# Streaming the high and low activation parts as one 512-column matmul in a two-part float32r trunk

## The chip, the cores and the metric

The kernel runs on one core of one Trainium2 chip, as one launch. The metric is the device time of that launch in microseconds (us); lower is better. Engines are named as in the profile: PE is TensorE's matmuls, PEld its weight loads, DVE is VectorE, ACT is ScalarE, POOL is GpSimd, SP issues most DMAs.

## The reference

Two layers of a decoder trunk over 256 tokens with 1024 features, in float32. Each layer is a half-step SwiGLU feed-forward, a mixer (dilated attention beside a gated linear recurrence), a cross-attention into 256 memory tokens, and a second half-step feed-forward; an RMS norm stands ahead of each and at the end.

```python
def swiglu(h, w_gu, w_down):
    gate, up = jnp.split(h @ w_gu, 2, axis=-1)
    return (jax.nn.silu(gate) * up) @ w_down
...
    for l in range(DEPTH):
        x = x + 0.5 * swiglu(rms_norm(x, ffn1_norm[l]), ffn1_w_gu[l], ffn1_w_down[l])
        h = rms_norm(x, mix_norm[l])
        z = h @ w_in[l]
        ...
        merged = jax.nn.sigmoid(gate_a) * y_a + jax.nn.sigmoid(gate_b) * y_b
        x = x + merged @ w_mix_out[l]
        x = x + cross_attention(rms_norm(x, xattn_norm[l]), rms_norm(mem, mem_norm[l]),
                                xattn_wq[l], xattn_wkv[l], xattn_wo[l])
        x = x + 0.5 * swiglu(rms_norm(x, ffn2_norm[l]), ffn2_w_gu[l], ffn2_w_down[l])
    return rms_norm(x, final_norm)
```

Nearly all arithmetic is in the products of 256 tokens with weight matrices: 67 million weights in all, each used once.

## The kernel before, in words

**Two-part arithmetic.** Every weight and every activation operand is held as a high part (the value rounded to float32r) and a low part (the rest). A product is three matmuls that add into the same place of PSUM: high by high, high by low, low by high (`mm3`).

**Weights.** All weights lie in DRAM as blocks of 128 x 128 in the order of their use. `Stream` loads them in chunks of 16 blocks (1 MB), and splits them in halves of 8 blocks: ACT casts a half to `whi` (L104), DVE subtracts to get `wlo` (L110). Each time that a half is begun, `take` prepares later halves and then calls `tick`.

**Two kinds of products.** A feature-major product (`fm`) keeps a 128 x 128 weight block standing in the array and streams a tile of activations, 128 features by 256 tokens; its output tile has 128 output features by 256 tokens. L259 is high weight by high activation, L260 the same high weight by the low activation, L261 low weight by high activation. There are 3840 weight blocks in such products. A token-major product (`tm`, L263 to L265) keeps activations standing and streams four weight blocks at once, 512 columns; there are 224 matmuls of each of its three lines.

**Order of the work around them.** The order is written by hand. `defer(n, f)` puts a function off by n ticks, that is by n halves; `sides` holds side work (the recurrence `hgrn`, the attention heads, cross-attention scores, memory norms), of which a tick runs one step; `urgent` holds the norms, and evictions queue behind it. So the stream of matmuls on PE is a row of `fm` and `tm` blocks with small groups of side matmuls between halves. `Act` keeps high and low parts of an operand in separate tiles. Most `fm` calls compute two output tiles of 16 blocks in all; the down projections one tile of 22 blocks.

**PSUM.** There are eight banks of 128 x 512, taken one at a time by `bank()`. An `fm` output tile uses the first 256 columns of a bank. The eviction reads it straight: in the feed-forward, DVE multiplies by the norm (L423, L425), ACT applies SiLU (L424), DVE multiplies (L428), ACT rounds (L243) and DVE subtracts (L246). L353 adds a product to the residual.

Of the kernel before, what the change touches and what calls it, by code (L numbers as in the profile page):

```python
# [46 lines left out]
class Stream:  # L47
    """Weight blocks of 128 x 128 in the order of their use: loaded in chunks, split in high and low parts."""
# [16 lines left out]
    def pieces(self, i, before=None):  # L65
        """Both parts of half i, by pairs of blocks."""
# [46 lines left out]
    def take(self, descs):  # L113
        """The parts of the next blocks, which lie side by side."""
# [13 lines left out]
def build(tc, a, nchunks):  # L128
# [11 lines left out]
    psum = ent(tc.tile_pool(name="psum", bufs=8, space=bass.MemoryType.PSUM))  # L140
# [7 lines left out]

    def bank():
        return psum.tile([P, 512], F32, name="bank")  # L150
# [68 lines left out]
    class Row:  # L219
        """Tiles of [128, 256], four to a slot; a slot is taken when it is first asked for."""  # L220
# [8 lines left out]

    class Act:  # L230
        """A feature-major operand in two parts; tile k holds features 128 k .. 128 k + 127 of all tokens."""

        def __init__(self):
            self.h, self.l = Row(F32R), Row(F32R)

        def hi(self, k):
            return self.h(k)

        def lo(self, k):
            return self.l(k)  # L240

        def put(self, k, src, later=0):
            nc.scalar.copy(self.hi(k), src)  # L243

            def low():
                nc.vector.tensor_tensor(self.lo(k), src, self.hi(k).bitcast(F32), op=OP.subtract)  # L246
# [29 lines left out]
    def fm(name, l, cols, act, K, evac):  # L276
        """Feature-major products: one output tile of 128 columns of the weight for each of cols."""
        banks = [bank() for _ in cols]
        for k in range(K):
            for c, b in zip(cols, banks):  # L280
                wh, wl = W.take([(name, l, k * P, c)])
                mm3(b[:, :T], wh, wl, act.hi(k), act.lo(k), k == 0, k == K - 1, True)
        after(lambda: evac(*[b[:, :T] for b in banks]))

    def tm(name, l, c, act, evac):
        """Token-major products: 512 columns of the weight, both tiles of tokens."""
        banks = [bank(), bank()]
# [54 lines left out]
    class Resid:  # L342
        """Takes the products that are added to the residual, and makes the next operand of them."""
# [6 lines left out]
        def take(self, j, *ps):  # L350
            js = range(j, j + len(ps))
            for j, p in zip(js, ps):
                nc.vector.scalar_tensor_tensor(xt[j], p, self.scale, xt[j], op0=OP.mult, op1=OP.add)  # L353
            for j in js:
                self.act.put_gain(j, xt[j], self.gain(j))
            for j in js:
                self.norm.add(xt[j])

    class Last:
        """Takes the last products, and returns the normed residual, token-major."""  # L360
# [5 lines left out]
        def take(self, j, p):  # L366
            nc.vector.scalar_tensor_tensor(xt[j], p, 0.5, xt[j], op0=OP.mult, op1=OP.add)
# [14 lines left out]
        def turn(self, j, g):  # L382
            for i in range(2):
                if (i, j // 4) not in self.b:
                    self.b[i, j // 4] = bank()
                nc.tensor.transpose(self.b[i, j // 4][:, (j % 4) * P:(j % 4 + 1) * P], g[:, i * P:(i + 1) * P], ident)

        def finish(self, g):
# [10 lines left out]
            for i in range(2):  # L399
                o = slot()  # L400
                nc.scalar.activation(o[:, :512], self.b[i, 0], AF.Copy, scale=r[:, i:i + 1])
                nc.vector.tensor_scalar(o[:, 512:], self.b[i, 1], r[:, i:i + 1], None, op0=OP.mult)
# [3 lines left out]
    def mm_resid(name, l, act, K, res):  # L406
        if K == KD:
            for j in range(0, KD, 2):
                fm(name, l, [j * P, (j + 1) * P], act, K,
                   lambda p, q, j=j: res.take(j, p, q))  # L410
        else:
            for j in range(KD):
                fm(name, l, [j * P], act, K, lambda p, j=j: res.take(j, p))

# [1 line left out]
    def ffn(pre, l, res, nxt):  # L416
# [3 lines left out]
        for j in range(KF):  # L420
            def evac(pg, pu, j=j):
                g, s, u = tmp(), tmp(), tmp()
                nc.vector.tensor_tensor(g, pg, n.bc, op=OP.mult)  # L423
                nc.scalar.activation(s, g, AF.Silu)  # L424
                nc.vector.tensor_tensor(u, pu, n.bc, op=OP.mult)  # L425

                def stage2():
                    nc.vector.tensor_tensor(u, s, u, op=OP.mult)  # L428
                    act.put(j, u, later=0 if j == KF - 1 else 1)
                if j == KF - 1:  # L430
                    stage2()
                else:
                    defer(1, stage2)
            fm(pre + "_w_gu", l, [j * P, FF + j * P], h, KD, evac)
# [86 lines left out]
    def hgrn(l, hh, Q, K, F, ib, sog, out):  # L521
# [63 lines left out]
        bs = []  # L585
        for i in range(2):
            b = bank()
            bs.append(b)
# [35 lines left out]
    def attention(l, h, qk, v, out):  # L624
        b0, b1, b2 = bank(), bank(), bank()
# [359 lines left out]
```

## Time and profile before

| | |
|---|---|
| time, median of 3 runs | 1681.54 us (1681.42 to 1681.98) |
| span of the profiled execution, first to last instruction | 1679.6 us |
| median less that span | 1.9 us |
| PE busy | 1666.9 us (99%) |
| DVE busy | 1120.2 us (67%) |
| ACT busy | 836.9 us (50%) |
| POOL busy | 63.8 us (4%) |

The table's own time for the profiled execution is its span; the time of a run is a little longer than the span. "Busy" of PE counts overlapping records of a pipeline (a matmul's record starts before the one ahead of it has ended), so the distance between starts, not the record's length, says how fast matmuls follow each other.

### The profile page before, as it was taken

How to read it: one execution, taken by the hardware profiler on the slowest of the kernel's cores; microseconds unless marked ns; L12 is line 12 of the kernel's file. 1: busy time of each engine (PE TensorE's matmuls, PEld its weight loads, DVE VectorE, ACT ScalarE, POOL GpSimd, SP SyncE). 2: the span in 40 equal slices, each digit the busy share in tenths (PEclk: the TensorE clock that was granted, in tenths of full speed). 3: DMA queues.
4: the chain of work that ended last, by engine and by line, in shares of the span. 5: the costliest groups of instructions: out<-in, count | busy, mean ns of one | idle time of the engine just before them, and what ended most of it. 6: DMA issues, size and time to landing. Idle time of an engine off the chain costs nothing.

```text
span 1679.6 us, 34164 instructions
## 1 busy us (share of the span) xinstructions
PE 1666.9 (99%) x14658; PEld 1625.1 (97%) x14658; DVE 1120.2 (67%) x1821; ACT 836.9 (50%) x1285; POOL 63.8 (4%) x85
## 2 busy tenths in 40 slices
PE   8999999999999999999999999999999999999998
PEld 8999998899999999999999999988999999999998
DVE  7766586667768667666566656867586777676654
ACT  5554435555555555444444444445565555554442
POOL 2000000111100000000000000010110000000000
PEclk9999999999999999999999999999999999999999
DMA  7544444444455445554545544444344554445551
GB/s 282 191 177 176 178 175 153 150 176 151 151 177 180 175 147 176 181 192 180 183 174 193 179 178 174 162 148 174 146 157 154 192 197 155 149 178 180 192 180 76
DMA packets 41767, 289.42 MB, mean 172 GB/s; under 512 B 4880, under 2 KB 5008, under 8 KB 7440
## 3 DMA queue, kind: packets, MB, share of 16 engines
q1 hardware_dynamic: 41328, 286.73, 47.6%
q8 instruction: 114, 1.87, 0.4%
q10 hardware_dynamic: 288, 0.52, 0.1%
q14 instruction: 37, 0.30, 0.0%
HBM read 286.18 MB, written 1.05 MB: 171 GB/s over the span
## 4 chain that ended last, share of the span: by engine, by line
PE 98%; DVE 1%; DMA 0%; SPq 0%; ACT 0%; issue 0%; POOLq 0%; POOL 0%; ACTq 0%; DVEq 0%
PE bank L259 28%; PE bank L261 28%; PE bank L260 28%; PE bank L263 3%; PE bank L265 3%; PE bank L264 3%; PE bank L547 1%; PE bank L669 1%; PE bank L632 1%; PE bank L592 0%; DMA raw<-w 0%; PE bank L628 0%; PE bank L671 0%; PE bank L329 0%; DVE wlo L77 0%; PE bank L836 0%
## 5 line engine op out<-in xcount | busy, mean ns | idle before, releaser
L259 PE MATMUL bank<-slot,whi 128*128 128x256 f32 x3840 | 1095.0, 285 | 0.0
L261 PE MATMUL bank<-slot,wlo 128*128 128x256 f32 x3840 | 1087.0, 283 | 2.9 <-DVE wlo L77 2.9
L260 PE MATMUL bank<-slot,whi 128*128 128x256 f32 x3840 | 1086.8, 283 | 0.0
L261 PEld LDWEIGHTS bank<-slot,wlo 128*128 128x128 f32 x3840 | 736.4, 192 | 4.1 <-DVE wlo L77 4.1
L260 PEld LDWEIGHTS bank<-slot,whi 128*128 128x128 f32 x3840 | 736.6, 192 | 1.3
L259 PEld LDWEIGHTS bank<-slot,whi 128*128 128x128 f32 x3840 | 736.5, 192 | 1.5
L110 DVE TENSOR_TENSOR wlo<-raw,whi 128x1024 fp32r<-128x1024 f32 x532 | 648.7, 1233 | 39.1 <-ACT whi L104 35.0
L104 ACT CAST whi<-raw 128x1024 fp32r<-128x1024 f32 x532 | 540.9, 1043 | 58.0 <-PE bank L260 23.9
L423 DVE TENSOR_TENSOR tmp<-bank,bc 128x256 f32<-128x256 f32 x88 | 37.4, 425 | 157.0 <-PE bank L261 153.0
L424 ACT ACTIVATE tmp<-tmp 128x256 f32<-128x256 f32 x88 | 36.8, 420 | 201.8 <-DVE tmp L423 201.8
L243 ACT CAST slot<-tmp 128x256 fp32r<-128x256 f32 x152 | 60.4, 407 | 109.2 <-DVE tmp L428 38.5
L253 ACT ACTIVATE slot<-x,vecs 128x256 fp32r<-128x256 f32 x64 | 30.8, 505 | 138.5 <-DVE x L353 136.3
L263 PE MATMUL bank<-whi,slot 128*128 128x512 f32 x224 | 90.0, 402 | 0.0
L265 PE MATMUL bank<-whi,slot 128*128 128x512 f32 x224 | 87.5, 390 | 0.0
L264 PE MATMUL bank<-wlo,slot 128*128 128x512 f32 x224 | 87.4, 390 | 0.0
L353 DVE SCALAR_TENSOR_TENSOR x<-bank,x 128x256 f32<-128x256 f32 x56 | 22.7, 425 | 85.6 <-PE bank L261 85.6
L760 DVE TENSOR_TENSOR slot<-bank,cosb 128x256 f32<-128x256 f32 x48 | 20.4, 425 | 64.4 <-ACT tmp L759 62.9
L246 DVE TENSOR_TENSOR slot<-tmp,slot 128x256 fp32r<-128x256 f32 x152 | 60.9, 419 | 2.8 <-ACT slot L243 2.8
L265 PEld LDWEIGHTS bank<-whi,slot 128*128 128x128 f32 x224 | 42.0, 188 | 9.2
L761 POOL TENSOR_TENSOR tmp<-tmp,sinb 128x256 f32<-128x256 f32 x48 | 35.4, 740 | 391.7 <-ACT tmp L759 390.7
L263 PEld LDWEIGHTS bank<-whi,slot 128*128 128x128 f32 x224 | 42.1, 188 | 8.3
L264 PEld LDWEIGHTS bank<-wlo,slot 128*128 128x128 f32 x224 | 42.2, 188 | 7.7
(178 smaller groups left out, 973.9 us busy)
## 6 DMA issues: line engine op xcount, KB each, us to landing
raw<-w SPq DMA_DIRECT2D x267, 1024.0 KB, 4.8
slot<-mem SPq DMA_DIRECT2D x6, 512.0 KB, 7.1
x<-x SPq DMA_DIRECT2D x4, 256.0 KB, 4.8
raw<-w SPq DMA_DIRECT2D x4, 256.0 KB, 5.2
cst<-cst SPq DMA_DIRECT2D x1, 721.0 KB, 11.6
y<-slot ACTq DMA_DIRECT2D x2, 256.0 KB, 2.8
y<-slot SPq DMA_DIRECT2D x2, 256.0 KB, 2.8
posi<-positions SPq DMA_DIRECT2D x1, 128.0 KB, 10.5
```

Source lines behind the costliest of these rows:

```text
L104: nc.scalar.copy(self.hi[i], r)
L110: nc.vector.tensor_tensor(self.lo[i], r, self.hi[i].bitcast(F32), op=OP.subtract)
L243: nc.scalar.copy(self.hi(k), src)
L246: nc.vector.tensor_tensor(self.lo(k), src, self.hi(k).bitcast(F32), op=OP.subtract)
L259: nc.tensor.matmul(out, wh, ah, start=first, stop=False)
L260: nc.tensor.matmul(out, wh, al, start=False, stop=False)
L261: nc.tensor.matmul(out, wl, ah, start=False, stop=last)
L263: nc.tensor.matmul(out, ah, wh, start=first, stop=False)
L264: nc.tensor.matmul(out, ah, wl, start=False, stop=False)
L265: nc.tensor.matmul(out, al, wh, start=False, stop=last)
L423: nc.vector.tensor_tensor(g, pg, n.bc, op=OP.mult)
L424: nc.scalar.activation(s, g, AF.Silu)
```

## The change

The two activation parts of a tile now lie side by side in a slot (`Act.parts`, 512 columns), and `fm` streams both past the standing high weight in one matmul of 512 columns (L320 of the new kernel). Its output fills a whole bank: the left half takes high by high, the right half high by low. The low weight then adds its product with the high activations to the left half (L321, 256 columns). The eviction has to add the two halves: `add_halves` copies the right half to SBUF on ACT (L327) at once, and one tick later DVE adds the left half to it (L330); what followed before (norm, SiLU and so on) now follows that sum, in joint operations of two tiles. For products that go to the residual, two scalar_tensor_tensor operations take the place of one. PSUM is handed out in four pairs of banks, and a `bank()` for side work takes a pair as well.

```diff
+    joins = ent(tc.tile_pool(name="joins", bufs=4))
-    psum = ent(tc.tile_pool(name="psum", bufs=8, space=bass.MemoryType.PSUM))
+    psum = ent(tc.tile_pool(name="psum", bufs=4, space=bass.MemoryType.PSUM))
...
+    def pair():
+        return psum.tile([P, 1024], F32, name="pair")
+
     def bank():
-        return psum.tile([P, 512], F32, name="bank")
+        return pair()[:, :512]
...
-    def fm(name, l, cols, act, K, evac):
-        banks = [bank() for _ in cols]
-        for k in range(K):
-            for c, b in zip(cols, banks):
-                wh, wl = W.take([(name, l, k * P, c)])
-                mm3(b[:, :T], wh, wl, act.hi(k), act.lo(k), k == 0, k == K - 1, True)
-        after(lambda: evac(*[b[:, :T] for b in banks]))
+    def fm(items, evac):
+        b = pair().rearrange("p (i h t) -> p i h t", i=2, h=2)
...
+        for k, i in order:
+            name, l, c, act, K = items[i]
+            wh, wl = W.take([(name, l, k * P, c)])
+            nc.tensor.matmul(b[:, i], wh, two(act.parts(k)), start=k == 0, stop=False)
+            nc.tensor.matmul(b[:, i, 0], wl, act.hi(k), start=False, stop=k == K - 1)
+        n = len(items)
+        after(lambda: evac(b[:, :n, 0], b[:, :n, 1]))
+
+    def add_halves(d, left, right, then, now=False):
+        nc.scalar.copy(d, right)
+        def add():
+            nc.vector.tensor_tensor(d, left, d, op=OP.add)
+            then()
+        if now:
+            add()
+        else:
+            defer(1, add)
...
-                nc.vector.scalar_tensor_tensor(xt[j], p, self.scale, xt[j], op0=OP.mult, op1=OP.add)
+            for half in (left, right):
+                nc.vector.scalar_tensor_tensor(x, half, self.scale, x, op0=OP.mult, op1=OP.add)
...
-                nc.vector.tensor_tensor(g, pg, n.bc, op=OP.mult)
-                nc.scalar.activation(s, g, AF.Silu)
-                nc.vector.tensor_tensor(u, pu, n.bc, op=OP.mult)
+                t, s = join(), tmp()
+                u = t[:, T:]
+                def stage1():
+                    nc.vector.tensor_tensor(two(t), two(t), both(n.bc), op=OP.mult)
+                    nc.scalar.activation(s, t[:, :T], AF.Silu)
...
+                add_halves(two(t), left, right, stage1, last)
```

On PE, inside any feed-forward product, two weight blocks stood like this before (`slot` is the activation operand, `whi` and `wlo` the weight parts):

```order
100 L259 MATMUL bank<-slot,whi 128x256
101 L260 MATMUL bank<-slot,whi 128x256
102 L261 MATMUL bank<-slot,wlo 128x256
103 L259 MATMUL bank<-slot,whi 128x256
104 L260 MATMUL bank<-slot,whi 128x256
105 L261 MATMUL bank<-slot,wlo 128x256
```

and the same two blocks stand like this in the changed kernel:

```order
78 L320 MATMUL pair<-slot,whi 128x512
79 L321 MATMUL pair<-slot,wlo 128x256
80 L320 MATMUL pair<-slot,whi 128x512
81 L321 MATMUL pair<-slot,wlo 128x256
```

Six matmuls with six weight loads have become four with four; the streamed columns, 768 a block, are the same.

On DVE, while the recurrence's first pass (`hgrn`, whose steps update Q and K in L553 and L554) runs between the products of the forget gate and the query (`recur`: L708, L710, L713, L714), one pair of output tiles came with these rows before:

```order
267 L708 TENSOR_TENSOR tmp<-bank,bc 128x256
268 L710 SCALAR_TENSOR_TENSOR slot<-bank,bc 128x256
269 L110 TENSOR_TENSOR wlo<-raw,whi 128x1024
270 L713 TENSOR_SCALAR slot<-tmp,oml,lb 128x256
271 L714 TENSOR_SCALAR slot<-slot 128x256
272 L553 TENSOR_TENSOR slot<-slot,tt 128x32x16
273 L554 TENSOR_TENSOR slot<-slot,tt 128x32x16
274 L557 TENSOR_TENSOR tt<-tt 128x32
275 L563 COPY_PREDICATED tmp<-cpm,bank 128x8x16
276 L110 TENSOR_TENSOR wlo<-raw,whi 128x1024
```

In the changed kernel the same pair's rows, here with the next step of the recurrence behind them, are these (L764, L766, L770, L771, L609, L610 and L613 are the old L708, L710, L713, L714, L553, L554 and L557):

```order
285 L330 TENSOR_TENSOR join<-pair,join 128x512
286 L764 TENSOR_TENSOR join<-join,bc 128x256
287 L766 SCALAR_TENSOR_TENSOR slot<-join,bc 128x256
288 L110 TENSOR_TENSOR wlo<-raw,whi 128x1024
289 L770 TENSOR_SCALAR slot<-join,oml,lb 128x256
290 L771 TENSOR_SCALAR slot<-slot 128x256
291 L609 TENSOR_TENSOR slot<-slot,tt 128x16x32
292 L610 TENSOR_TENSOR slot<-slot,tt 128x16x32
293 L613 TENSOR_TENSOR tt<-tt 128x16
```

The pair has one more DVE row, the addition of 512 columns out of PSUM, and the four others have moved back by one half of weights.

On ACT, a feed-forward pair stood like this before (L104 casts weights, L307 squares for the memory norm):

```order
58 L307 ACTIVATE tmp<-slot 128x256
59 L424 ACTIVATE tmp<-tmp 128x256
60 L104 CAST whi<-raw 128x1024
61 L243 CAST slot<-tmp 128x256
62 L104 CAST whi<-raw 128x1024
```

and stands like this now (L360, L480 and L275 are the old L307, L424 and L243):

```order
66 L360 ACTIVATE tmp<-slot 128x256
67 L327 COPY join<-pair 128x512
68 L104 CAST whi<-raw 128x1024
69 L480 ACTIVATE tmp<-join 128x256
70 L104 CAST whi<-raw 128x1024
71 L275 CAST slot<-join 128x256
```

The copy of the right halves is new and stands ahead of the weight cast; SiLU has moved behind that cast.

## Rows read from the trace of the kernel before

**Rows 1.** The page: span, busy engines, and the chain's shares by engine.

```profile
span 1679.6 us, 34164 instructions
...
PE 1666.9 (99%) x14658; PEld 1625.1 (97%) x14658; DVE 1120.2 (67%) x1821; ACT 836.9 (50%) x1285; POOL 63.8 (4%) x85
...
PE 98%; DVE 1%; DMA 0%; SPq 0%; ACT 0%; issue 0%; POOLq 0%; POOL 0%; ACTq 0%; DVEq 0%
```

**Rows 2.** All waits of PE: who waited for whom, us in total, times, longest.

```profile
PE bank L261 <- DVE wlo L77: 2.9, 6, 0.5
PE bank L209 <- ACT warm L206: 2.3, 1, 2.3
PE bank L393 <- ACT tmp L372: 0.8, 1, 0.8
```

**Rows 3.** Timeline of PE in the feed-forward: start, duration in us, line, shape.

```profile
799.74 0.28 PE L260 MATMUL bank<-slot,whi 128*128 128x256 f32 x1
...
805.98 0.28 PE L261 MATMUL bank<-slot,wlo 128*128 128x256 f32 x1
```

**Rows 4.** Timeline of PE in a token-major product, and where it ends.

```profile
262.12 0.40 PE L264 MATMUL bank<-wlo,slot 128*128 128x512 f32 x1
...
265.98 0.39 PE L263 MATMUL bank<-whi,slot 128*128 128x512 f32 x1
...
270.09 0.39 PE L265 MATMUL bank<-whi,slot 128*128 128x512 f32 x1
270.31 0.28 PE L259 MATMUL bank<-slot,whi 128*128 128x256 f32 x1
270.43 0.28 PE L260 MATMUL bank<-slot,whi 128*128 128x256 f32 x1
```

**Rows 5.** Timeline of PE: attention scores in plain float32, six records merged.

```profile
326.28 1.46 PE L632 MATMUL bank<-slot 128*128 128x256 f32 x6
```

**Rows 6.** Groups by line and shape: busy us, mean ns of one, idle before.

```profile
L259 PE MATMUL bank<-slot,whi 128*128 128x256 f32 x3840 | 1095.0, 285 | 0.0
...
L110 DVE TENSOR_TENSOR wlo<-raw,whi 128x1024 fp32r<-128x1024 f32 x532 | 648.7, 1233 | 39.1 <-ACT whi L104 35.0 <-PE bank L261 2.0 <-issue 1.4
...
L423 DVE TENSOR_TENSOR tmp<-bank,bc 128x256 f32<-128x256 f32 x88 | 37.4, 425 | 157.0 <-PE bank L261 153.0 <-ACT bc L331 4.0
...
L605 DVE TENSOR_TENSOR slot<-bank,rs 128x512 f32<-128x512 f32 x8 | 5.1, 681 | 0.0
...
L660 ACT COPY slot<-bank 128x512 f32<-128x512 f32 x8 | 4.7, 584 | 9.8 <-PE bank L657 9.6
```

**Rows 7.** Busy us of PE, PEld, DVE, ACT, POOL in stretches; clock, DMA share, GB/s.

```profile
37.00:47.00 10.00, 10.00 (x85) 10.00 (x84) 7.85 (x15) 4.88 (x7) 0.00 (x0) 1.00 0.48 170
...
212.00:482.00 270.00, 269.99 (x2750) 254.96 (x2749) 188.71 (x305) 137.44 (x213) 21.95 (x28) 1.00 0.44 158
...
235.00:239.00 4.00, 4.00 (x136) 3.84 (x133) 3.97 (x9) 2.31 (x3) 0.00 (x0) 1.00 0.21 88
239.00:243.00 4.00, 4.00 (x126) 3.80 (x114) 4.00 (x9) 0.44 (x2) 0.00 (x0) 1.00 0.43 111
```

**Rows 8.** Timeline of DVE through one pair of the recurrence's products.

```profile
234.61 0.42 DVE L708 TENSOR_TENSOR tmp<-bank,bc 128x256 f32<-128x256 f32 x1 [1.15 <-PE bank L261]
...
237.70 0.69 DVE L554 TENSOR_TENSOR slot<-slot 128x512 f32<-128x512 f32 x1
238.30 0.68 DVE L557 TENSOR_TENSOR tt<-slot 128x512 f32<-128x512 f32 x1
...
242.07 0.45 DVE L708 TENSOR_TENSOR tmp<-bank,bc 128x256 f32<-128x256 f32 x1
```

**Rows 9.** The chain of work that ended last, at a step of the recurrence.

```profile
238.66 0.67 PE bank L547 x52
```

**Rows 10.** Timelines: PE's last paced matmul at the start; the last residual update.

```profile
16.64 0.38 PE L261 MATMUL bank<-slot,wlo 128*128 128x256 f32 x1 [0.49 <-DVE wlo L77]
...
1671.00 0.42 DVE L367 SCALAR_TENSOR_TENSOR x<-bank,x 128x256 f32<-128x256 f32 x1 [6.53 <-PE bank L261]
```

More of the change, by code (lines that the diff above doesn't have):

```diff
@@ L147, in tmp, with join, two, both @@
         return tmps.tile([P, T], F32, name="tmp")
+    def pair():
+        return psum.tile([P, 1024], F32, name="pair")
     def bank():
-        return psum.tile([P, 512], F32, name="bank")
+        return pair()[:, :512]
+    def join():
+        return joins.tile([P, 2 * T], F32, name="join")
+    def two(t):
+        return t.rearrange("p (i t) -> p i t", i=2)
+    def both(t):
+        return t[:, None].to_broadcast([P, 2, T])
     deferred, sides, flags = [], [], set()
@@ L348, in __init__, with take @@
             self.gain, self.scale = gain, scale
-        def take(self, j, *ps):
-            js = range(j, j + len(ps))
-            for j, p in zip(js, ps):
-                nc.vector.scalar_tensor_tensor(xt[j], p, self.scale, xt[j], op0=OP.mult, op1=OP.add)
[L354 to L357, printed above, removed]
+        def take(self, j, left, right):
+            n = left.shape[1]
+            x = xall[:, j * T:(j + n) * T].rearrange("p (i t) -> p i t", i=n)
+            for half in (left, right):
+                nc.vector.scalar_tensor_tensor(x, half, self.scale, x, op0=OP.mult, op1=OP.add)
+            for i in range(j, j + n):
+                self.act.put_gain(i, xt[i], self.gain(i))
+            for i in range(j, j + n):
+                self.norm.add(xt[i])
     class Last:
@@ L364, in __init__, with take @@
             self.b = {}
-        def take(self, j, p):
-            nc.vector.scalar_tensor_tensor(xt[j], p, 0.5, xt[j], op0=OP.mult, op1=OP.add)
+        def take(self, j, left, right):
+            for half in (left, right):
+                nc.vector.scalar_tensor_tensor(xt[j], half[:, 0], 0.5, xt[j], op0=OP.mult, op1=OP.add)
             if j == 0:
@@ L406, in mm_resid @@
     def mm_resid(name, l, act, K, res):
[L407 to L413, printed above, removed]
+        n = 2 if K == KD else 1
+        for j in range(0, KD, n):
+            fm([(name, l, (j + i) * P, act, K) for i in range(n)],
+               lambda left, right, j=j: res.take(j, left, right))
     def ffn(pre, l, res, nxt):
@@ L624, in attention @@
     def attention(l, h, qk, v, out):
-        b0, b1, b2 = bank(), bank(), bank()
+        b0, b1 = bank(), pair()
         for g in range(NG):
@@ L777, in gate, with sigmoid @@
-            fm("w_in", l, [CGA + j * P, CGB + j * P], h, KD, evac)
+            def sigmoid():
+                for t in gates.t.values():
+                    nc.scalar.activation(t, t, AF.Sigmoid)
+            fm([("w_in", l, c + j * P, h, KD) for c in (CGA, CGB)],
+               lambda left, right: scaled(gates.two(2 * j), left, right, sigmoid if j == KD - 1 else None))
         for u in range(HH):
```

204 lines of the change are left out of this document (111 added, 93 removed).

## Prediction

> **What bounds the kernel now.** The page comes first: PE is busy 1666.9 of 1679.6 us, and 98% of the chain that ended last is PE [rows 1]. DVE (67%) and ACT (50%) are far from it over the whole. Busy time alone would not settle it, since PE's records overlap, so the waits come next: PE waited for three things only, 2.9 + 2.3 + 0.8 = 6.0 us in all, the first weights, the first warm-up and the last norm [rows 2]. In between it never stands still. The question for this change is then only how far apart matmuls start, and whether something new makes PE wait.
>
> The distance between starts is read from the timeline. In the feed-forward 52 steps of 256 columns take 805.98 - 799.74 = 6.24 us, 0.120 us each, though each record is 0.28 us long [rows 3]. In a token-major product 17 steps of 512 columns take 3.86 us, 0.227 us each [rows 4]. Twice the columns cost 0.107 us more, which is 256 columns at 2.4 GHz; so each matmul with its weight load carries about 0.0135 us that has nothing to do with its columns. Where the two widths meet, the step behind a 512-column matmul is 0.22 us (270.09 to 270.31) [rows 4]: the width of the matmul ahead sets the step.
>
> **The change, part by part.**
>
> *The matmuls.* A weight block took three steps of 256 columns, 3 x 0.120 = 0.360 us. It now takes one of 512 and one of 256: 0.227 + 0.120 = 0.347 us. The saving is 0.013 us a block, and 3840 blocks [rows 6] make 49.9 us. The first twelve or so save nothing, since PE is paced by DVE's split of the first weights until 16.64 us [rows 10]; that is 0.2 us. The gain is 49.7 us. No row shows exactly the new form, a standing weight with 512 streamed activation columns: the 512-column rows of before have activations standing and weights streaming. Both stream float32r out of SBUF into one bank; I take 0.227. The bounds: no surplus at all beyond the columns, 0.213, would be worth 0.014 x 3840 = 54 us more, but no 512-column row goes below 0.22; and a surplus that grows with the columns, 0.240, takes the whole gain away (second rival).
>
> The Trainium skill, "TensorE: Matmul & The Clock Gate", section "Back-to-back issue gap", speaks against a gain of this size: it gives a warm isolated gap of N/2.4 + 2.5 ns, by which a merged matmul would save 2.5 ns a block, an estimated 9.6 us in all. The trace does not agree for float32r (0.120 and 0.227 us, not 0.109 and 0.216).
>
> *The eviction.* Each two-tile `fm` gains an ACT copy of 512 columns out of PSUM (like L660, 0.584 us) and a DVE addition of 512 out of PSUM (like L605, 0.681) [rows 6]. Records on DVE overlap by some 0.08 us: 237.70 to 238.30 is a step of 0.60 for a 0.69 record [rows 8]. In a feed-forward pair DVE had about 0.34 + 0.34 + 0.34 (L423 and its like, 0.425 less that overlap) for the norm and the product with SiLU; now 0.60 + 0.60 + 0.34, that is 0.5 us more, and ACT 0.58 more. The stretch with 7.85 of 10 us on DVE and 4.88 on ACT [rows 7] holds under two pairs: it goes to about 8.8 and 5.9 of 9.65. Over the program, 184 such joins add about 110 us to DVE and as much to ACT, so about 75% and 58% of a span of 1637. This lies beside PE's work and costs nothing while PE doesn't need its result at once. In the feed-forward it doesn't: four pairs in turn mean that a pair is taken again three `fm`, 3 x 16 x 0.347 = 16.7 us, after its addition was issued, and the last tile of the down projection's operand is not asked for until 21 blocks, 7.3 us, into the first down product.
>
> *Where the cover is thin.* (a) The recurrence's first pass. One pair of products took 242.07 - 234.61 = 7.46 us on DVE without a gap [rows 8], DVE is full from 235 to 243 [rows 7], and the next step of the recurrence (L547, on PE) needs DVE's L554: that ends 238.39, PE starts at 238.66 [rows 8, 9]. The slack is 0.27 us. The pair now has 0.6 us more on DVE, and PE's period shrinks by 16 x 0.013 = 0.2 us. The lag is 0.8 us in the first full pair, about 0.2 in the two that follow, because the later steps are smaller. Behind PE's wait everything is queued, the weight blocks too. Per layer 0 to 3.2 us (four pairs at 0.8; nothing if the 1.15 us idle ahead of the stretch [rows 8] absorbs it); I take 1.5, 3 us for both layers.
> (b) Pairs of banks. Side work takes one of four pairs where it took one of eight banks. By the changed order, in the mixer and the cross-attention a pair is taken again 2 to 3 us of PE work after its last reader was issued, at about seven places a layer. The reader is a copy and an addition in line, 0.58 + 0.68 = 1.27 us, and with one weight split of 1.23 us ahead of it (L110) [rows 6] 2.5 us. So the wait is 0 to 1 us each, 0 to 14 us; most have no split ahead; I take 3 us.
> (c) Nine norms, whose broadcast comes one half after its statistics; a half is 8 x 0.013 = 0.1 us shorter, and the same chain of DVE and POOL must fit. 0 to 0.1 us each without other lag, up to 0.4 with a late addition ahead: 0 to 3.6; I take 1.
> (d) The end. The last update of the residual, 0.42 us (L367) [rows 10], becomes two in line, with nothing to hide it: 0.4 us.
> (e) The branch products, where joins and the memory operand meet on DVE: 0 to 3; I take 1.
>
> *The sum.* Against the profiled execution: 1679.6 - 49.7 + 3 + 3 + 1 + 0.4 + 1 = 1638.3 us of span. The median of the runs lies 1.9 us above that execution's span (1681.54 less 1679.6); the same added gives 1640.2. With all of (a) to (e) at their low ends it is 1632, at their high ends 1659.
>
> **The rivals.**
>
> *DVE sets the mixer's pace.* The joins add about 16 us a layer to DVE between the mixer's norm and its branch products, where it has 188.7 of 270 us [rows 7]. If the bunching of attention, recurrence and evictions turned every added microsecond there and some 4 in the branch products into a PE wait, 2 x 20 = 40 us would come back: 1632 + 40 = 1672. For it: DVE is full in the stretch of (a). Against it: 81 us of its time are idle in these 270, and weights are split two halves ahead. A part of this, 10 to 40 us over my sum of losses, gives 1649 to 1671. Chance 0.12.
>
> *The surplus grows with the columns in the new form* (the other side). A step of 0.240 us behind a 512-column matmul with standing weights would leave 0.360 us a block, and the losses alone would show: 1681.5 + 8.4 = 1690. It decides where 0.013 us a block becomes 8.4/3840 = 0.002: at a step of 0.238. Against it: 0.227 in every 512-column row, and 0.22 at the seam with standing weights [rows 4]. Chance 0.05.
>
> *Most of the surplus stays with the block.* In plain float32 six records follow each other in (1.46 - 0.38)/5 = 0.216 us [rows 5], just over 512 columns' worth, each with a weight load of its own. So a load need not cost 0.0135 us; if the greater part belonged to the change of a block's two weight parts, the merge would save 0.0027 us a block, 10 us, which the losses eat: 1681.5 - 10 + 8.4 = 1680. Against it: the step from L259 to L260, which keeps the same weight, is 0.12 [rows 4] like the mean of all [rows 3]. Chance 0.03. The rule of the Trainium skill above ("TensorE: Matmul & The Clock Gate", "Back-to-back issue gap") would come to about this time.
>
> **How the numbers follow.** My forecast, 1633 to 1649, has 0.80. Its middle term gives the time, 1640. The range of 8 in 10 takes its low end with all losses at nothing, 1632, and reaches into the first rival to 1658. A measurement of this kernel tells 0.2%, 3.4 us, from no change; the forecast and the first rival are faster (0.92), the third is the same (0.03), the second slower (0.05).
>
> **What would show it.** In the feed-forward, starts at 0.227 and 0.120 us in turn, blocks at 0.347. No wait of PE on an addition (L330) in the feed-forward; in the mixer waits of PE on DVE's L609, L610 and L330 of some tenths each, a few us in all. DVE near 1230 us and ACT near 945 busy. The prediction is wrong if the blocks come at another distance, or if PE's waits add up to more than 20 us.

## The result, and the profile after

The changed kernel takes 1673.12 us (median of 4 runs, 1671.91 to 1673.63) beside 1681.75 us (1681.42 to 1681.98) for the kernel before on the same chip: a ratio of 0.9948, with a 95% interval of 0.9934 to 0.9962. It is faster, by 8.6 us where 41 were forecast, and the time lies outside the predicted range of 1632 to 1658. The runs of the kernel after spread over 1.7 us where those of before spread over 0.6.

The page of the kernel after (an execution of 1671.91 us, 1.8 us of which lie outside its span), with the lines that answer to those of before [rows 1]:

```profile
span 1670.1 us, 26491 instructions
...
PE 1638.0 (98%) x10818; PEld 1417.4 (85%) x10818; DVE 1243.2 (74%) x1813; ACT 924.5 (55%) x1389; POOL 77.3 (5%) x61
...
PE 77%; DVE 11%; issue 8%; ACT 2%; POOL 1%; DMA 1%; SPq 0%; POOLq 0%; ACTq 0%; DVEq 0%
```

PE has 3840 matmuls less and is still the engine that is busy nearly all the time. That its share of the chain falls from 98% to 77% says little here: in the fastest kernel below, where PE waits half as long, the chain gives it 78%. The waits are what to read. All waits of PE in the kernel after that last more than 0.3 us in all (who waited for whom, us in total, times, longest), where [rows 2] had three lines and 6.0 us:

```profile
PE pair L320 <- DVE slot L278: 7.2, 2, 4.3
PE pair L321 <- DVE wlo L110: 3.9, 2, 2.0
PE pair L648 <- ACT tt L652: 2.7, 4, 0.7
PE pair L382 <- DVE tmp L377: 2.4, 6, 0.7
PE pair L222 <- ACT warm L219: 2.3, 1, 2.3
PE pair L321 <- DVE wlo L77: 1.6, 5, 0.3
PE pair L448 <- ACT tmp L427: 1.3, 1, 1.3
PE pair L603 <- DVE slot L610: 0.9, 3, 0.4
PE pair L368 <- DVE tmp L362: 0.7, 1, 0.7
PE pair L670 <- DVE tmp L675: 0.6, 2, 0.3
```

These ten make 23.6 us. The first two, 11.1 us, are four waits: low parts of a merged tile (L278) and of weights (L110). Counted along PE's blocks, all four stand in the branch products and early in mix-out (after its first 12 blocks), two in each layer. But 17.6 us more waiting does not make up what is missing: 49.7 us were to be gained and 8.6 came. So the distance between starts comes next.

**Two paces.** The timeline of PE in two stretches of the feed-forward of the kernel after (start, duration in us, line, shape), the first of 9 blocks, the second of 11:

```profile
119.77 0.28 PE L321 MATMUL pair<-slot,wlo 128*128 128x256 f32 x1
119.89 0.39 PE L320 MATMUL pair<-slot,whi 128*128 128x512 f32 x1
120.12 0.28 PE L321 MATMUL pair<-slot,wlo 128*128 128x256 f32 x1
...
122.89 0.28 PE L321 MATMUL pair<-slot,wlo 128*128 128x256 f32 x1
```

```profile
799.81 0.28 PE L321 MATMUL pair<-slot,wlo 128*128 128x256 f32 x1
799.93 0.40 PE L320 MATMUL pair<-slot,whi 128*128 128x512 f32 x1
800.17 0.28 PE L321 MATMUL pair<-slot,wlo 128*128 128x256 f32 x1
800.29 0.40 PE L320 MATMUL pair<-slot,whi 128*128 128x512 f32 x1
...
800.64 0.40 PE L320 MATMUL pair<-slot,whi 128*128 128x512 f32 x1
...
800.99 0.40 PE L320 MATMUL pair<-slot,whi 128*128 128x512 f32 x1
...
803.70 0.28 PE L321 MATMUL pair<-slot,wlo 128*128 128x256 f32 x1
```

3.12 us over 9 blocks is 0.3467 us a block; 3.89 over 11 is 0.3536. Nothing waits in either stretch, and the granted clock is 1.00 in both (below). The kernel before knew one distance, 0.120 three times [rows 3]. Each pace is a pattern, seen in all the starts of the trace: the short one alternates blocks of 0.343 and 0.350 us, the long one goes round in threes, 0.349, 0.350 and 0.361 (799.93, 800.29, 800.64, 800.99 above). The pace holds for long stretches, mostly whole stages: the first feed-forward of both layers runs at the short one, the second almost wholly at the long one. Over the 3627 blocks that follow each other without a break the mean is 0.3498 us: 0.0031 above 0.3467, which makes 11.2 us. The step inside a block is not as predicted either: at the short pace 0.232 us follow the 512-column matmul and 0.115 the 256-column one, where 0.227 and 0.120 were put together. Their sum, 0.347, is right at the short pace. (By the Trainium skill, "TensorE: Matmul & The Clock Gate", section "Back-to-back issue gap", which gives the gap of a single warm matmul, the two would make 512/2.4 + 256/2.4 + 2 x 2.5 ns, an estimate of 0.325 us; neither pace agrees.)

**The half clock.** Windows of the kernel after over the branch products and mix-out of the first layer, the two stretches of above, and the second layer (busy us of PE, PEld, DVE, ACT, POOL; granted clock; DMA share; GB/s):

```profile
505.20:507.50 2.30, 0.42 (x3) 0.10 (x1) 2.02 (x4) 2.30 (x6) 0.00 (x0) 1.00 0.00 0
507.90:511.40 3.50, 3.50 (x13) 2.96 (x12) 3.43 (x6) 1.11 (x2) 0.00 (x0) 0.51 0.73 283
521.40:524.60 3.20, 0.27 (x3) 0.04 (x1) 2.70 (x6) 2.30 (x3) 0.00 (x0) 1.00 0.08 33
524.60:528.50 3.90, 3.90 (x13) 3.39 (x14) 2.31 (x3) 0.00 (x0) 0.00 (x0) 0.56 0.39 143
119.77:122.89 3.12, 3.12 (x19) 2.73 (x18) 1.94 (x5) 1.57 (x3) 0.00 (x0) 1.00 0.78 315
799.81:803.70 3.89, 3.89 (x23) 3.38 (x22) 3.09 (x4) 2.18 (x3) 0.00 (x0) 1.00 0.20 36
...
1343.70:1348.10 4.40, 0.24 (x2) 0.00 (x0) 3.72 (x7) 2.41 (x4) 0.00 (x0) 0.95 0.35 147
1348.20:1351.10 2.90, 2.87 (x9) 2.51 (x10) 1.02 (x1) 0.00 (x0) 0.00 (x0) 0.50 0.17 40
```

Read them in pairs: PE is idle for 1.9, 2.9 and 4.3 us, and when it works again, or shortly after, its granted clock is 0.50, the lower of its two levels (1.2 GHz), for 3.4, 3.4 and 2.9 us of its work (a mean of 0.51 over 3.50 us and of 0.56 over 3.90 us hold 3.4 us of it each). A busy PE hides it on the page: 3.50 of 3.50 us busy, with 13 matmuls where the full clock fits 20. In the timeline the blocks come 0.64 us apart there (four from 508.24 to 510.81). The fourth such wait, 2.0 us that ended at 1331.19, was not followed by a slow stretch. Over the traces of all kernels here the waits of 2.4 to 4.9 us were followed by one each time, ten of ten, those of 1.7 to 2.0 us five times of eight; what decides between these is open. (The Trainium skill, same page, part "The HAM clock gate", says that an idle PE falls to half its clock and comes back after sustained work; the trace agrees that it falls and comes back, 0.50 and then 1.00.) 9.7 us at half clock are 15 blocks at 0.64 instead of 0.35, so some 4.4 us are lost there on top of the waits.

**Where 51 us went.** The matmuls at the short pace would have taken 51.1 us off (3840 blocks at 0.0133 us). From the starts of the matmuls with low weight parts in the two traces, stage by stage: the loss is a stage's time after, less its time before lessened by 0.0133 us a block. All of it, 41.6 us in both layers, explains why 9.5 came off the span (1679.6 to 1670.1) and not 51.1 (the rows are rounded).

| stage | blocks, both layers | loss, us |
|---|---|---|
| first feed-forward | 1056 | 1.5 |
| recurrence's first pass | 256 | 0.8 |
| rest of the mixer up to the branch products | 768 | 9.5 |
| branch products | 192 | 7.6 |
| mix-out | 128 | 10.7 |
| cross-attention | 384 | 3.5 |
| second feed-forward, with the end | 1056 | 8.1 |

Branch products and mix-out lose 18.3 us on 8% of the blocks: about 11.8 in the four waits (counted from start to start of matmuls, less a usual step), 4.4 at half clock, and little waits and the pace in the rest.

**What is late there.** The timelines of ACT and DVE in the kernel after, at the first of the four waits (504.63 to 507.42; PE restarts at 507.56):

```profile
504.63 0.41 ACT L275 CAST slot<-join 128x256 fp32r<-128x256 f32 x1 [2.43 <-DVE join L868]
504.94 0.90 ACT L285 ACTIVATE slot<-slot,vecs 128x256 fp32r<-128x256 f32 x2
505.75 1.03 ACT L104 CAST whi<-raw 128x1024 fp32r<-128x1024 f32 x1
```

```profile
505.48 0.88 DVE L286 SCALAR_TENSOR_TENSOR slot<-slot,vecs 128x256 fp32r<-128x256 f32 x2 [0.89 <-ACT slot L285]
506.28 1.22 DVE L110 TENSOR_TENSOR wlo<-raw,whi 128x1024 fp32r<-128x1024 f32 x1
```

ACT's cast of a merged tile (L275) waits 2.43 us for DVE's last addition of that tile (L868). Behind it in ACT's order stand the memory operand's high parts (L285) and a cast of weights (L104). DVE in turn is idle for 0.89 us until the first of these high parts is there (L286 waits for L285). Behind that, in DVE's order, stands the split of weights (L110) that PE needs: it starts at 506.28, before the cast at 505.75 has ended, so it is not that cast that it waited for. Work on a merged tile goes ACT (copy out of the bank, L327), DVE (L330, L866, L868), ACT (L275), DVE (L278); before the change it had no copy and no ACT ahead of DVE. Two engines that each work in order now wait for each other in turn (the crossing, below), and the weights stand in both queues.

The wait in mix-out is another one. The same kernel's DVE and PE at 522.55 to 524.59:

```profile
522.55 0.43 DVE L278 TENSOR_TENSOR slot<-join,slot 128x256 fp32r<-128x256 f32 x1 [0.47 <-ACT slot L275]
522.89 1.22 DVE L110 TENSOR_TENSOR wlo<-raw,whi 128x1024 fp32r<-128x1024 f32 x1
524.03 0.42 DVE L278 TENSOR_TENSOR slot<-join,slot 128x256 fp32r<-128x256 f32 x1
```

```profile
524.59 0.47 PE L320 MATMUL pair<-slot,whi 128*128 128x512 f32 x1 [2.93 <-DVE slot L278]
```

PE has done 12 blocks of mix-out, those on the first six merged tiles, and now needs the seventh. The program subtracts the eighth tile at once (522.55) and puts the seventh off to the next half of weights (the argument `later` of `mg.put`), so its subtraction (524.03) stands behind the whole chain of the eighth tile and a weight split.

### The profile page after: what moved, and what is told of

Same layout as the page of the kernel before. It is cut to its first block, busy times and chain, and to the rows that moved or that the text cites. A ratio compares the mean times of both kernels' runs of the same rounds, so it can differ in the third digit from the quotient of the medians.

```text
span 1670.1 us, 26491 instructions
## 1 busy us (share of the span) xinstructions
PE 1638.0 (98%) x10818; PEld 1417.4 (85%) x10818; DVE 1243.2 (74%) x1813; ACT 924.5 (55%) x1389; POOL 77.3 (5%) x61
## 4 chain that ended last, share of the span: by engine, by line
PE 77%; DVE 11%; issue 8%; ACT 2%; POOL 1%; DMA 1%; SPq 0%; POOLq 0%; ACTq 0%; DVEq 0%
PE pair L320 41%; PE pair L321 21%; DVE wlo L110 4%; PE pair L295 3%; PE pair L297 3%; PE pair L296 3%; PE pair L603 1%; DVE join L330 1%; DVE slot L286 1%; DVE join L866 1%; PE pair L688 1%; PE pair L722 1%; DVE x L407 1%; DMA raw<-w 1%; PE pair L648 0%
## 5 line engine op out<-in xcount | busy, mean ns | idle before, releaser
L320 PE MATMUL pair<-slot,whi 128*128 128x512 f32 x3840 | 1362.0, 399 | 8.2 <-DVE slot L278 7.2
L321 PE MATMUL pair<-slot,wlo 128*128 128x256 f32 x3840 | 1077.0, 280 | 5.6 <-DVE wlo L110 3.9
L320 PEld LDWEIGHTS pair<-slot,whi 128*128 128x128 f32 x3840 | 724.1, 189 | 179.1 <-ACT whi L104 7.8
L321 PEld LDWEIGHTS pair<-slot,wlo 128*128 128x128 f32 x3840 | 727.1, 189 | 9.7 <-DVE wlo L110 5.2
L110 DVE TENSOR_TENSOR wlo<-raw,whi 128x1024 fp32r<-128x1024 f32 x532 | 641.1, 1221 | 40.4 <-ACT whi L104 39.7
L104 ACT CAST whi<-raw 128x1024 fp32r<-128x1024 f32 x532 | 545.6, 1046 | 24.0 <-issue 9.5
L330 DVE TENSOR_TENSOR join<-pair,join 128x512 f32<-128x512 f32 x136 | 93.8, 689 | 108.4 <-ACT join L327 108.3
L327 ACT COPY join<-pair 128x512 f32<-128x512 f32 x136 | 79.4, 585 | 171.7 <-PE pair L321 171.7
L285 ACT ACTIVATE slot<-x,vecs 128x256 fp32r<-128x256 f32 x64 | 30.8, 505 | 141.8 <-DVE x L407 139.3
L295 PE MATMUL pair<-whi,slot 128*128 128x512 f32 x224 | 89.8, 401 | 0.0
L297 PE MATMUL pair<-whi,slot 128*128 128x512 f32 x224 | 87.6, 391 | 0.0
L296 PE MATMUL pair<-wlo,slot 128*128 128x512 f32 x224 | 87.5, 391 | 0.0
L275 ACT CAST slot<-join 128x256 fp32r<-128x256 f32 (+1 forms) x120 | 51.9, 435 | 52.5 <-DVE join L868 30.6
L480 ACT ACTIVATE tmp<-join 128x256 f32<-128x256 f32 x88 | 36.6, 418 | 54.6 <-DVE join L479 54.6
L327 ACT COPY slot<-pair 128x512 f32<-128x512 f32 x48 | 28.0, 583 | 67.8 <-PE pair L321 67.8
L479 DVE TENSOR_TENSOR join<-join,bc 128x512 f32<-128x512 f32 x88 | 60.9, 692 | 3.0
L330 DVE TENSOR_TENSOR slot<-pair,slot 128x512 f32<-128x512 f32 x48 | 33.1, 689 | 35.6 <-ACT slot L327 35.6
L278 DVE TENSOR_TENSOR slot<-join,slot 128x256 fp32r<-128x256 f32 (+1 forms) x120 | 54.0, 454 | 2.8 <-ACT slot L275 2.8
L286 DVE SCALAR_TENSOR_TENSOR slot<-x,vecs,slot 128x256 fp32r<-128x256 f32 x64 | 31.9, 520 | 27.1 <-ACT slot L285 27.0
## 6 DMA issues: line engine op xcount, KB each, us to landing
cst<-cst SPq DMA_DIRECT2D x1, 721.0 KB, 11.8
```

Of the source, the lines that this page charges most:

```text
L104: nc.scalar.copy(self.hi[i], r)
L110: nc.vector.tensor_tensor(self.lo[i], r, self.hi[i].bitcast(F32), op=OP.subtract)
L278: nc.vector.tensor_tensor(l, src, h.bitcast(F32), op=OP.subtract)
L295: nc.tensor.matmul(out, ah, wh, start=first, stop=False)
L296: nc.tensor.matmul(out, ah, wl, start=False, stop=False)
L297: nc.tensor.matmul(out, al, wh, start=False, stop=last)
```

## The experiments

All are against the kernel before on the same chip as the run; the median of that was 1681.58 to 1681.65 us.

**1. Branch products as before** (three 256-column matmuls, eviction by DVE alone), all else as in the kernel after.

```
-            fm([("w_att_branch", l, j * P, aout, AH), ("w_hgrn_branch", l, j * P, hout, HH)], evac)
...
+            for name, act, K, d in (("w_att_branch", aout, AH, pa), ("w_hgrn_branch", hout, HH, pb)):
+                for k in range(K):
+                    wh, wl = W.take([(name, l, k * P, j * P)])
+                    mm3(d, wh, wl, act.hi(k), act.lo(k), k == 0, k == K - 1, True)
+            def evac(pa=pa, pb=pb, j=j):
...
+                nc.vector.tensor_tensor(m1, pa, gates(2 * j), op=OP.mult)
+                nc.vector.tensor_tensor(m2, pb, gates(2 * j + 1), op=OP.mult)
+                nc.vector.tensor_tensor(m1, m1, m2, op=OP.add)
...
```

> Only the branch products (192 of 3840 blocks) go back to three 256-column matmuls and to the eviction of before, which reads PSUM straight. In the changed kernel the branch and the mix-out product behind it lose 18.2 us over both layers against 0.0133 us saved a block. Theory A, DVE is overloaded there by the joins: nearly all of that comes back, less 2.6 us of saving given up on 192 blocks: about 1657 us (1654 to 1661). Rival B, the loss there has another cause (the pairs of banks, the memory operand alone): 1670 to 1676 us.

Measured: 1657.95 us (1655.2 to 1658.83), ratio 0.9856 [0.9841, 0.9871]. In its trace (the execution of 1655.2 us) the four waits are gone, the granted clock stays at 1.00 from the start to the last norm, and mix-out loses nothing (22.2 us a layer where 22.2 were due). Two other executions, 1658.55 and 1658.83 us, had a mean clock of 0.996 instead of 0.999, so in them the clock fell at a place that no trace shows. Undoing the change on a twentieth of the blocks gives 15 us.

**2. The 512-column matmul in two halves of 256,** with the new evictions and pairs of banks: the merge alone is undone.

```
-            nc.tensor.matmul(b[:, i], wh, two(act.parts(k)), start=k == 0, stop=False)
+            nc.tensor.matmul(b[:, i, 0], wh, act.hi(k), start=k == 0, stop=False)
+            nc.tensor.matmul(b[:, i, 1], wh, act.lo(k), start=False, stop=False)
```

> The 512-column matmul is split again into two of 256 columns (high by high, high by low), everything else as in the changed kernel, so the evictions are tested without the merge. Theory on the pace, the two paces of a block (0.347 and 0.353 us) come from the alternation of 512 and 256 columns: steps of 0.120 us everywhere, blocks at 0.360, one pace only. Rival, the slower pace comes from the eviction's traffic: stretches of blocks above 0.360. Time: 1673 + 51 for the merge - 11 for the slower pace that is gone - about 10 because PE is then slower than DVE in the branch products: about 1703 us (1695 to 1708).

Measured: 1703.57 us (1703.08 to 1704.97), ratio 1.0131 [1.0116, 1.0147]. All blocks are 0.360 us apart, as before. So evictions and pairs alone cost 22 us and the merge gives 30 back: the prediction had 8.4 and 49.7. The same waits for L278 and L110 stand here (6.2 and 3.4 us), so they come of the eviction and not of a faster PE.

**3. Two 512-column matmuls, then their two 256-column ones,** over two blocks at a time.

```
-        for k, i in order:
+        for u in range(0, len(order), 2):
+            for k, i in order[u:u + 2]:
...
+                nc.tensor.matmul(b[:, i], wh, two(act.parts(k)), start=k == 0, stop=False)
+                lows.append((i, wl, act.hi(k), k == K - 1))
+            for i, wl, h, last in lows:
+                nc.tensor.matmul(b[:, i, 0], wl, h, start=False, stop=last)
```

> Blocks are taken two by two: both 512-column matmuls first, then both 256-column ones; the same work. Theory on the pace, a stream that alternates 512 and 256 columns block by block locks into one of two phases at each restart: with the new order a pair of blocks takes 0.6933 us everywhere and the 11 us of slower pace come back: about 1662 us. Rival, the pace is set by something else (addresses, traffic of other engines): slow stretches stay, about 1673 us.

Measured: 1668.12 us (1667.42 to 1668.96), ratio 0.992 [0.9905, 0.9934]. Both paces give way to one, 0.348 us a block in every feed-forward stage: the second feed-forward loses 3.9 us instead of 8.1, the first 2.5 instead of 1.5. The expected 1662 needed 0.3467 everywhere; 0.0015 a block stays.

**4. The memory operand's low parts on POOL,** to relieve DVE in the branch products.

```
-                hm.put_gain(j, m(j), vec("mem_norm", l, j))
+                hm.put_gain_pool(j, m(j), vec("mem_norm", l, j))
```

The new function multiplies by the gain and subtracts the high part in two operations on POOL (L292, L293 below).

> The low parts of the memory operand, which DVE makes during the branch products (8 operations of 0.45 us a layer), are made by POOL in two operations each. Theory A1, DVE has more work in the branch products than PE (34.2 us against 33.3): with 3.6 us less the loss in branch and mix-out falls from about 9 to under 4 us a layer: about 1662 us. Rival A2, the last join's chain (copy, add, product, add, cast, subtract in line) is what PE waits for, whatever else DVE does: the loss stays at 7 us or more a layer, 1670 us or more. POOL and DVE may slow each other, which would show in longer durations of both.

Measured: 1669.2 us (1668.1 to 1674.26), ratio 0.9936 [0.9919, 0.9952]. The branch products lose 1.0 us a layer, but mix-out 6.9. Waits of PE, and groups of POOL and DVE (busy, mean ns) in 478 to 546 us, of this kernel:

```profile
PE pair L326 <- DVE slot L278: 9.8, 2, 4.9
```

```profile
L292 POOL TENSOR_SCALAR tmp<-slot,vecs 128x256 f32<-128x256 f32 x8 | 12.1, 1516 | 31.9 <-DMA slot<-mem 31.9
L293 POOL TENSOR_TENSOR slot<-tmp,slot 128x256 fp32r<-128x256 f32 x8 | 8.4, 1046 | 12.8 <-ACT slot L290 12.2
...
L278 DVE TENSOR_TENSOR slot<-join,slot 128x256 fp32r<-128x256 f32 x8 | 4.8, 601 | 0.5 <-ACT slot L275 0.5
```

The stops inside the products are gone, and nearly all of the waiting is now in mix-out, for the seventh tile. And DVE's own subtraction takes 0.601 us on average in this stretch, where it takes 0.420 in the kernel after (the same line, 8 times, 3.4 us): four of the eight lie within POOL's operations and take 0.61 or 0.95 us, the other four 0.42. With POOL at work beside it this operation is slower. (The Trainium skill, "GPSIMD Engine Reference", "Specifications", says that GpSimd shares its SBUF interfaces with VectorE; this row agrees.) So the relief was partly taken back. And the edit takes out of DVE's order just the operation that waited for ACT (L286), so the run does not tell DVE's load from the order of the queues by itself.

**5. The joined branch products taken out of the bank by DVE alone,** without ACT's copy.

```
-                add_halves(two(t), left, right, stage1, last)
+                nc.vector.tensor_tensor(two(t), left, gates.two(2 * j), op=OP.mult)
+                nc.vector.tensor_tensor(two(u), right, gates.two(2 * j), op=OP.mult)
+                nc.vector.tensor_tensor(t, t, u, op=OP.add)
...
```

> The branch products keep the joined 512-column matmuls, but VectorE alone takes the two halves out of the bank (left times gate, right times gate, one add of 512 columns, then the add of the two products): ScalarE's copy and VectorE's wait for it are gone, and VectorE works 0.68 us more on each of 16 tiles (0.685 for the second product out of the bank, 0.692 for the add, less one of these that was there). Theory A, the branch loses because ScalarE's copy and cast and VectorE's adds wait for each other in turn, each in its engine's order: loss of branch and mix-out together falls from 9.2 us a layer to 3 or less, time near 1660 us. Theory B, VectorE simply has more work there than TensorE's stretch holds: loss grows by up to 5.4 us a layer, time 1678 to 1684.

Measured: 1671.8 us (1668.54 to 1674.37), ratio 0.9941 [0.9926, 0.9956]: between the two, and not apart from the kernel after. The branch products lose 7.0 us a layer instead of 4.5 and 3.1, mix-out 2.2 instead of 4.7 and 5.9. That fits a last tile that is ready sooner without the copy (theory A's half) and tiles before it that are later with 0.68 us more on DVE (theory B's). The waits of ACT in 478 to 546 us in this kernel show that the crossing was not removed:

```profile
ACT slot L275 <- DVE join L867: 21.9, 8, 3.1
```

In the kernel after the same cast waits 15.3 us for L868. ACT waits for DVE even longer, and the cast of the weights still stands behind it.

**6. Only the place of that cast:** it is issued one tick later, and with it the subtraction behind it.

```
-                    mg.put(j, m, later=0 if last else 1)
+                    if last:
+                        mg.put(j, m)
+                    else:
+                        defer(1, lambda: mg.put(j, m, later=1))
```

> Only the place of the cast that rounds a merged tile is changed: it is issued one tick later, so that in ScalarE's order about half of the copies of the next tile's right halves, the last tile's among them, stand ahead of the cast that waits for VectorE instead of behind it. No work is added or taken. Theory A (the two engines' queues cross): loss of branch and mix-out falls from 9.2 us a layer to about half, time 1663 to 1666. Theory B (VectorE has too much work): the same work, so no change, 1673.

Measured: 1668.24 us (1664.97 to 1669.72), ratio 0.9918 [0.9903, 0.9933]. The interval ends just below where that of the kernel after begins, and every run lies below all of that kernel's; the time lies between the two theories. With the same work on every engine the branch products now lose 0.6 us a layer: PE does not stop. Mix-out still waits, and loses 6.3 us a layer instead of 5.3. Windows of this kernel:

```profile
480.00:513.70 33.70, 33.70 (x192) 29.19 (x191) 28.23 (x43) 24.89 (x38) 0.00 (x0) 1.00 0.45 162
518.80:523.00 4.20, 0.13 (x2) 0.00 (x0) 3.70 (x6) 2.60 (x4) 0.00 (x0) 0.96 0.21 88
523.80:525.90 2.10, 2.10 (x8) 1.81 (x7) 0.00 (x0) 0.00 (x0) 0.00 (x0) 0.50 1.01 281
```

DVE is busy 28.2 of 33.7 us and PE never waits: so DVE's load does not make the waits inside the branch products; the order in the two queues does. The wait behind them has the other cause: the chain of six steps for the last two tiles, one tile behind the other on DVE, is longer than the 12 blocks that mix-out can do without them, and PE's clock falls behind it again. The edit makes this wait longer, 4.26 us instead of 2.93, since it puts the seventh tile's subtraction off by one more half, behind two weight splits. DVE in this kernel:

```profile
520.11 0.43 DVE L278 TENSOR_TENSOR slot<-join,slot 128x256 fp32r<-128x256 f32 x1 [0.47 <-ACT slot L275]
520.45 2.35 DVE L110 TENSOR_TENSOR wlo<-raw,whi 128x1024 fp32r<-128x1024 f32 x2
522.72 0.42 DVE L278 TENSOR_TENSOR slot<-join,slot 128x256 fp32r<-128x256 f32 x1
```

No run takes that subtraction out from behind the splits, so how much of the wait is this order and how much the chain is not shown.

**7 and 8. Together:** 1 and 3; then also the recurrence's second pass with a pair of banks for each of its two value products.

```
-        both_tiles = pair()
-        bs = [both_tiles[:, :512], both_tiles[:, 512:]]
+        bs = [bank(), bank()]
```

> Two edits that were measured alone, together: branch products as three 256-column matmuls with the old eviction (1657.95 alone) and two 512-column matmuls and then their two 256-column ones (1668.12 alone, 5.0 less than the change as it is). If the two losses are apart, the gains add: 1652.9. If the pace and the stalls trade against each other (a faster TensorE waits more): 1656 or more.

> The kernel of the run before it with one more edit: the value products of the recurrence's second pass take a pair of banks each again instead of the halves of one. The four waits of PE for ScalarE's squares there, 0.9 us each in the kernel after, should go: 3.4 us less than the run before it, near 1649.5. If the one more pair taken makes a later product wait for its banks, the gain is eaten up: no difference, or slower.

Measured: 1651.81 us (1651.69 to 1652.1), ratio 0.9823 [0.9809, 0.9838], and 1650.06 us (1649.7 to 1650.23), ratio 0.9812 [0.9796, 0.9828]. The gains of 1 and 3 add. The third edit gives 1.75 us, half of what was expected (the expectation counted 0.9 us a wait, the view above 0.7): in the last run PE no longer waits for ACT's squares, the line of L648 is gone from its waits, and the rest of the mixer loses 6.5 us instead of 9.5 in the kernel after. It is the fastest kernel here. Its page:

```profile
PE 1628.9 (99%) x11010; PEld 1422.3 (86%) x11010; DVE 1233.1 (75%) x1813; ACT 917.1 (56%) x1373; POOL 77.0 (5%) x61
...
PE 78%; DVE 11%; issue 8%; ACT 2%; POOL 1%; DMA 0%; SPq 0%; POOLq 0%; ACTq 0%; DVEq 0%
```

**9. Four 512-column matmuls, then four of 256 columns,** on the kernel of experiment 8 (its `2` made `4`).

> The kernel of 1650.06 with four 512-column matmuls in a row and then their four 256-column ones, instead of two and two. There a pair of blocks takes about 0.697 us where its matmuls at their shortest distances make 0.693. Theory turn: what is left comes once at each turn between the two kinds of matmul, so that half as many turns leave half of it, about 0.9 ns less a block on some 3500 blocks: 1647. Theory block: it comes with each block, whatever the order: 1650, no difference.

Measured: 1655.97 us (1655.5 to 1656.83), ratio 0.985 [0.9833, 0.9866]: both theories fall, it is 6 us slower than two and two. The timelines of PE over 22 blocks of the first down products, first this kernel, then that of experiment 8:

```profile
161.18 1.08 PE L322 MATMUL pair<-slot,whi 128*128 128x512 f32 x4
...
168.88 1.08 PE L322 MATMUL pair<-slot,whi 128*128 128x512 f32 x4
```

```profile
166.49 0.63 PE L322 MATMUL pair<-slot,whi 128*128 128x512 f32 x2
...
174.15 0.62 PE L322 MATMUL pair<-slot,whi 128*128 128x512 f32 x2
```

7.70 us are 0.350 a block, 7.66 are 0.348. In this trace a 256-column matmul that follows another one starts 0.118 us behind it on average, nearly the 0.120 of before [rows 3], and 0.115 us behind it in experiment 8. What a matmul costs beyond its columns depends on more than its neighbour; I can't say on what.

**10. Joined branch products in six of eight tiles,** cast one tick later, three 256-column matmuls in the last two; else as experiment 8.

```
+            if j >= KD - 2:
+                b = pair()
...
+                after(evac)
+            else:
...
+                            defer(1, lambda: mg.put(j, m, later=1))
```

> The kernel of 1650.06 with joined 512-column matmuls in six of the eight tiles of the branch products (cast issued a tick later, as in the run before it that tried this), and three 256-column ones with the old eviction in the last two tiles alone, on which mix-out's start waits. If the losses there are the crossing of the two queues and the long chain behind the last tiles, both are gone, and 144 blocks gain 0.012 us each: 1648.5. If VectorE's longer work (2.2 us a tile instead of 1.7) still puts it behind at the end of the stretch, mix-out waits again and TensorE's clock falls: 1652 or more.

Measured: 1651.91 us (1651.34 to 1651.97), ratio 0.9823 [0.9809, 0.9838]: no gain over 8. The branch products gain 1.0 us a layer over it, mix-out gives 1.1 back and the cross-attention behind it 0.5. PE's clock does not fall. So it seems that even without joins in the last tiles something of the longer work on the joined ones arrives behind them: PE waits 0.4 us in both layers for L278, which it does not in the kernel of experiment 8. Where the rest of the 1.6 us a layer comes from is not shown.

## Why the prediction was wrong

*The matmuls.* The kind of gain was right, its size too large. The step "0.227 + 0.120 = 0.347 us" holds for the short pace alone; with the rest at 0.3536 the mean is 0.3498, so that the blocks gained 0.0102 us each, some 39 us and not 49.7. The error was to join two steps that had been read where one width streams for long, and to take the sum for the one value of the new alternation: [rows 3, 4] can't show that it has two. Experiments 2 and 3 show that it is the order of the two widths that brings them, since 256 columns alone have one pace and two-and-two has one. Why a stretch falls into the one or the other stays open; it is not tied to the stage, since in the run of experiment 1 the gate and up products of the last feed-forward lost 0.7 us where they lose 2.9 in the kernel after, with the same code there.

*(e), the branch products.* This is the term that failed most: 1 us (0 to 3) was taken, without a row or a working, and branch products with mix-out lost 18.3. It named the join and the memory operand on DVE alone. It did not see that the join puts ACT ahead of DVE and behind it again for the same tile, with the memory operand and the split of the weights behind both (experiment 6 shows that the order alone makes the stops inside the products), nor that behind PE's last branch product the two last tiles still need their six steps, and the seventh tile's last step stands behind weight splits as well, longer than the 12 blocks that mix-out can do without them (the trace after, experiments 1 and 6). The 4.4 us at half clock had no term at all: each wait was priced at its length.

*(a), the recurrence's first pass.* 3 us were taken, 0.8 were lost, near its low end: L603 waits for L610 three times, 0.9 us in all, the kind of wait that was named. What failed there is what the list did not have: the second pass, whose two value products came to share a pair of banks, so that the second product's matmuls waited for ACT's squares of the first (L648 behind L652, 2.7 us in four waits, [rows 2] without it). Experiment 8 got 1.75 us back by undoing it.

*(b) and (c).* Pairs: the transposes (L670) wait 0.6 us in two waits, below the 3 us taken. Norms: L382 waits 2.4 us six times and L368 0.7, so 3.1 where 1 was taken, inside 0 to 3.6. *(d)*: PE's wait at the end is 1.3 us where [rows 2] has 0.8 for the same step, 0.5 instead of 0.4.

*The rivals.* DVE as the mixer's pace: the time is near its band (1649 to 1671; 10 to 40 us over the sum of 1640 would be 1650 to 1680, which holds it), but not by its mechanism. DVE is busy 1243 us, close to the 1230 forecast, the rest of the mixer loses 9.5 us and not 32, and experiment 6 lets PE run with DVE at 28.2 of 33.7 us. The surplus that grows with the columns did not come: both paces are below 0.360, though every third block of the long one, at 0.361, is not. The third rival, most of the surplus with the block, would have made blocks of 0.357; both paces are shorter.

*Its own marks.* Blocks at 0.347: for about half of them. No wait for L330 in the feed-forward: held. Waits of PE above 20 us: 23.6, and by that mark the prediction was to be called wrong.

## What to carry to other kernels

Before joining two results on a second engine, write down in which order each engine takes its work around the join, and look whose loads stand behind the operation that will wait: a crossing of two in-order queues stops PE with both engines below full (DVE 31.1 and ACT 26.1 us in the 37.8 of the first layer's branch products). Price a wait of PE as long as those here with the half clock behind it, and look at the granted clock by windows, since the page's tenths hide it. A new alternation of matmul widths is to be measured in its own order: here its slower pace took back 11 of 50 us.

## What was unexpected of the hardware

A fixed order of a 512- and a 256-column float32r matmul, each with its own weight load, ran at two paces at full granted clock, 0.3467 and 0.3536 us a block, each kept for long stretches; in twos there was one, 0.348, and in fours 0.350 in the product shown. Waits of 1.9, 2.9 and 4.3 us were followed by 2.9 to 3.4 us of work at a granted clock of 0.50, one of 2.0 us was not. A subtraction on DVE took 0.61 or 0.95 us instead of 0.42 while POOL worked beside it.
